# Causal attention in groups of four: values one run of turns later, half moves by GpSimd copies, the scaling multiplication one event earlier

## The chip, the cores and the metric

One Trainium2 chip, one core. The metric is the device time of one execution in microseconds (us); lower is better. Times before come from three timed runs, and one further execution was profiled.

## The reference

One layer of a decoder: half a SwiGLU feed-forward step, a mixing step of three branches, half a second feed-forward step. There are 1024 positions of width 1024, all in float32. The change lies in branch B, causal attention with 8 heads, 96 query and key dimensions and 64 value dimensions:

```python
def one_block(args):
    i, qi = args
    s = jnp.einsum('bqhd,bkhd->bhqk', qi, k).astype(jnp.float32) * scale
    qpos = i * Q_BLOCK + jnp.arange(Q_BLOCK)
    mask = kpos[None, :] <= qpos[:, None]
    s = jnp.where(mask[None, None], s, NEG)
    p = jax.nn.softmax(s, axis=-1)
    return jnp.einsum('bhqk,bkhd->bqhd', p.astype(v.dtype), v)
```

## The kernel before

Float32 products are made of split numbers: a matrix is cut into a high part (`hi`, an ACT copy with rounding) and a low part (`lo`, the rest, a subtraction on DVE or POOL); `split` on L139 and L142 does both.

The attention works head by head on blocks of 128 positions. Query blocks are taken in two groups of four: group 0 is blocks 0 to 3 and group 1 is blocks 4 to 7. The steps are:

- R, one step of `prepare`: four transposes of queries or keys on PE (L450) into a PSUM bank, evicted by ACT (L150) and DVE (L151). Four such steps serve a head. For each pair of heads two 768 KB tiles, `ak` and `aq`, are loaded (L972).
- S or N, `scores` of one query block: PE writes the products into a tile `mm` (two of these exist, L158 to L160), DVE adds the mask and finds the extreme (L998), and ACT takes the exponential with its sum (L1001) into `pr`.
- T, `turn` of one key block: up to four transposes of `pr` (L1011) into one PSUM `bank` (there are four, which R and the value sums use too), evicted by `split` into `whi` (ACT) and `wlo` (DVE). For the last key block of a group POOL clears a corner (L1016).
- V, `value` of one key block: two matmuls (L1027, with `whi` and with `wlo`) that add to one bank over the whole group. The weights hold the values' high and low halves side by side, so the upper and the lower 64 rows of the sum must be added.
- `close`, after the last value of a group: ACT copies the sum to a tile `t` (L1043), the half that sits in the wrong rows is moved (L1044), and POOL adds the other half (L1045) into `ysum`, which gathers two heads. For an odd head DVE takes the reciprocals of the softmax sums (L1048). They go to DRAM as 4 KB (L1063, `invd`) and come back spread over 64 rows each (L1065, two loads to a tile `t`). A function put into the list `late` multiplies `ysum` by them on POOL (L1068) and splits the result: `x<-ysum` on ACT (L139) and POOL (L142). `late` counts events, that is, closes of a group.

A "cycle" of a head is written out by hand in `cycle(h)`; in it group 1 of the head before (TB, VB) and group 0 of this head (TA, VA) are interleaved with scores. Only PE follows the written order exactly. For the other engines and the DMA queue on SP, a scheduler fixes an order when the program is built; each engine then runs its own list in order and waits on semaphores.

## Time and profile before

| | |
|---|---|
| three timed runs | 2209.91, 2211.65 (median), 2212.57 us |
| profiled execution | 2212.67 us, span in the trace 2210.9 us |
| TensorE busy | 2175.1 us (98%), mean granted clock 0.994 |
| attention cycles | about 1251 to 1446 us of the span |

The span is cut off from the time by 1.77 us around it. In the trace each row has a start, a duration, an engine, a line and, in brackets, how long the engine had been idle before it and what ended that. PE's busy time runs to the modelled end of each matmul, so some waiting hides in it.

### The profile page before, as it was taken

To read this page: it belongs to the slowest core of one execution; us is meant where nothing else is said; L and a number is where in the kernel's file an instruction comes from. 1 tells how busy PE (TensorE), PEld (TensorE's weight loads), DVE (VectorE), ACT (ScalarE), POOL (GpSimd) and SP (SyncE) were. 2 spreads that over 40 slices of the span, in tenths; PEclk is the share of its full clock that TensorE was granted. 3 is DMA by queue.
4 is the path that set the end of the run, shared out by engine and by line. 5 is a ranking of instruction groups with operands and counts; after the bars stand their busy time and mean duration, and the time that the engine had idled before them with its cause. 6 is when DMAs were issued, how large, how long until landed. Compare 5 with 4: busy or idle time off the path is not lost.

```text
span 2210.9 us, 27223 instructions
## 1 busy us (share of the span) xinstructions
PE 2175.1 (98%) x9984; PEld 1798.6 (81%) x9984; DVE 1557.5 (70%) x2350; ACT 907.5 (41%) x1485; POOL 272.6 (12%) x244
## 2 busy tenths in 40 slices
PE   9999999999999999999999988899999999999999
PEld 6888888888888888888888766778888888888887
DVE  7976666589898666665976566585886666657884
ACT  6433333343455344433555366543442222224332
POOL 0011111100000000000313322240011121210000
PEclk9999999999999999999999999899999999999999
DMA  4265555684443445532786712175033333338543
GB/s 144 93 225 175 185 172 186 224 309 147 143 148 138 146 172 183 196 132 72 271 318 229 261 49 51 39 279 197 29 114 101 100 115 100 115 107 299 175 129 105
DMA packets 140870, 352.25 MB, mean 159 GB/s; under 512 B 22208, under 2 KB 30528, under 8 KB 140736
## 3 DMA queue, kind: packets, MB, share of 16 engines
q1 hardware_dynamic: 140592, 350.51, 46.5%
q8 instruction: 78, 1.28, 0.2%
q14 instruction: 56, 0.46, 0.1%
q10 hardware_dynamic: 144, 0.00, 0.0%
HBM read 235.62 MB, written 113.01 MB: 158 GB/s over the span
## 4 chain that ended last, share of the span: by engine, by line
PE 92%; DVE 3%; DMA 2%; ACT 1%; issue 1%; POOL 1%; SPq 0%; POOLq 0%; ACTq 0%; DVEq 0%
PE one L158 15%; PE one L159 15%; PE one L160 15%; PE bank L158 13%; PE bank L159 13%; PE bank L160 13%; PE bank L1027 2%; PE mm L158 1%; PE mm L159 1%; PE mm L160 1%; PE bank L1011 1%; DMA ysum<-t 1%; DVE wlo L142 1%; PE one L1982 1%; PE bank L1982 0%
## 5 line engine op out<-in xcount | busy, mean ns | idle before, releaser
L146 ACT CAST whi<-x 128x1024 fp32r<-128x1024 f32 x202 | 192.2, 955 | 405.0 <-DVE x L1452 162.5
L147 DVE TENSOR_TENSOR wlo<-x,whi 128x1024 fp32r<-128x1024 f32 x202 | 236.8, 1173 | 72.1 <-DMA wkv<-wlo 25.1
L1486 DVE TENSOR_TENSOR t<-t,one 128x512 f32<-128x512 f32 x188 | 128.9, 686 | 182.2 <-PE one L160 182.0
L158 PE MATMUL bank<-h,whi 128*128 128x512 f32 x636 | 248.1, 390 | 0.0
L160 PE MATMUL bank<-h,wlo 128*128 128x512 f32 x636 | 247.6, 389 | 0.0
L159 PE MATMUL bank<-h,whi 128*128 128x512 f32 x636 | 247.5, 389 | 0.0
L158 PE MATMUL one<-h,whi 128*128 128x512 f32 x508 | 198.9, 392 | 0.0
L160 PE MATMUL one<-h,wlo 128*128 128x512 f32 x508 | 198.3, 390 | 0.0
L159 PE MATMUL one<-h,whi 128*128 128x512 f32 x508 | 198.1, 390 | 0.0
L158 PE MATMUL one<-w,whi 128*128 128x512 f32 x432 | 168.5, 390 | 0.0
L160 PE MATMUL one<-w,wlo 128*128 128x512 f32 x432 | 168.1, 389 | 0.0
L159 PE MATMUL one<-w,whi 128*128 128x512 f32 x432 | 168.1, 389 | 0.0
L142 DVE TENSOR_TENSOR wlo<-w,whi 128x1024 fp32r<-128x1024 f32 (+2 forms) x112 | 114.4, 1037 | 65.4 <-ACT whi L139 65.1
L139 ACT CAST whi<-w 128x1024 fp32r<-128x1024 f32 (+2 forms) x112 | 98.8, 902 | 150.1 <-PE one L159 63.9
L2082 POOL TENSOR_TENSOR raw<-raw 128x512 f32<-128x512 f32 x38 | 57.0, 1499 | 796.2 <-DVE raw L1923 702.8
L160 PEld LDWEIGHTS bank<-h,wlo 128*128 128x128 f32 x636 | 119.4, 188 | 25.0
L158 PEld LDWEIGHTS bank<-h,whi 128*128 128x128 f32 x636 | 119.4, 188 | 24.6
L159 PEld LDWEIGHTS bank<-h,whi 128*128 128x128 f32 x636 | 119.4, 188 | 24.5
L158 PE MATMUL bank<-whi 128*128 128x512 f32 x352 | 136.9, 389 | 0.0
L159 PE MATMUL bank<-wlo,whi 128*128 128x512 f32 x352 | 136.9, 389 | 0.0
L160 PE MATMUL bank<-whi,wlo 128*128 128x512 f32 x352 | 136.9, 389 | 0.0
L160 PEld LDWEIGHTS one<-h,wlo 128*128 128x128 f32 x508 | 95.6, 188 | 20.0
(409 smaller groups left out, 4885.6 us busy)
## 6 DMA issues: line engine op xcount, KB each, us to landing
x<-in_ffn_w_gu_dram SPq DMA_DIRECT2D x78, 512.0 KB, 5.1
w<-tdt SPq DMA_DIRECT2D x40, 512.0 KB, 4.5
gate<-raw SPq DMA_DIRECT2D x33, 512.0 KB, 3.0
tdb<-raw SPq DMA_DIRECT2D x64, 256.0 KB, 2.3
h<-in_ffn_w_down_dram SPq DMA_DIRECT2D x64, 256.0 KB, 6.0
w<-tdb SPq DMA_DIRECT2D x30, 512.0 KB, 4.6
tdt<-w SPq DMA_DIRECT2D x48, 256.0 KB, 2.6
x<-in_w_gate_dram SPq DMA_DIRECT2D x22, 512.0 KB, 6.9
```

The costliest lines, as they stand in the source:

```text
L139: i = self.nc.scalar.copy(hi, src)
L142: return (eng or self.nc.vector).tensor_tensor(lo, src, hi.bitcast(F32), op=ALU.subtract)
L146: self.nc.scalar.copy(hi, src)
L147: return lambda: self.nc.vector.tensor_tensor(lo, src, hi.bitcast(F32), op=ALU.subtract)
L158: i = mmul(out, s[0], m[0], start=first, stop=False, **kw)
L159: mmul(out, s[0], m[1], start=False, stop=False, **kw)
L160: self.last = mmul(out, s[1], m[0], start=False, stop=last, **kw)
L1011: nc.tensor.transpose(b[:, t * P:(t + 1) * P], st[h, 4 * g + t][:, kk * P:(kk + 1) * P], self.ident)
L1027: nc.tensor.matmul(o[:, at:], w, x, start=kk == k == 0, stop=kk == 4 * g + 3 and k == 1, skip_group_check=True)
L1486: return self.nc.vector.tensor_tensor(out, x, y, op=ALU.add)
L1982: k.last = nc.tensor.matmul(b, w, norm.x(half, c), start=c == 0, stop=c == DT - 1)
L2082: sub = lambda d, x, y: (eng or nc.gpsimd).tensor_tensor(d, x, y, op=ALU.subtract)
```

## The change

Three edits:

- the half move L1044 is a GpSimd (POOL) copy from one half of the partitions to the other, in place of a DMA on SP's queue (14 of them: heads 0 to 6, two groups; head 7 has another path);
- the `late` function is cut in two: the multiplication is put out after two events and the split after three, where both stood at three;
- in `cycle` each run of values stands behind the next run of turns (or scores), not behind its own.

```diff
                     both = self.row()
                     nc.scalar.copy(both, o)
-                    nc.sync.dma_start(ys[rows], both[other])
+                    nc.gpsimd.tensor_copy(ys[rows], both[other])
                     nc.gpsimd.tensor_tensor(ys[rows], ys[rows], both[rows], op=ALU.add)
...
-                    def scale(y=yt[h // 2], cols=slice(g * 4 * P, (g + 1) * 4 * P)):
-                        nc.gpsimd.tensor_tensor(ys, ys, w, op=ALU.mult)
-                        self.split(y[0][:, cols], y[1][:, cols], ys, None if end else nc.gpsimd)
-
-                    late.append((0 if end else 3, scale))
+                    y, cols = yt[h // 2], slice(g * 4 * P, (g + 1) * 4 * P)
+                    late.append((0 if end else 2, lambda: nc.gpsimd.tensor_tensor(ys, ys, w, op=ALU.mult)))
+                    late.append((0 if end else 3, lambda: self.split(
+                        y[0][:, cols], y[1][:, cols], ys, None if end else nc.gpsimd)))
...
-                    *R(2), *TB(0, 1), *S(4), *VB(0, 1), *TB(2, 3, 4), *S(5), *VB(2, 3, 4), *TB(5, 6, 7), *S(6), *VB(5, 6, 7),
-                    *R(1), *TA(0, 1), *S(7), *VA(0, 1), *R(1), *TA(2, 3), *N(0, 1), *VA(2, 3), *N(2, 3)]
+                    *R(2), *TB(0, 1), *S(4), *TB(2, 3, 4), *S(5), *VB(0, 1), *TB(5, 6, 7), *S(6), *VB(2, 3, 4),
+                    *R(1), *TA(0, 1), *S(7), *VB(5, 6, 7), *R(1), *TA(2, 3), *N(0, 1), *VA(0, 1), *N(2, 3), *VA(2, 3)]
```

On PE, at the end of the first cycle: the rows with `h_10301` to `h_10304` are the values of key blocks 0 to 3, those with `mm` are scores of the next head (N).

```order
 L159 MATMUL mm<-h_10527,h_10524 128x256
 L160 MATMUL mm<-h_10526,h_10525 128x256
-L1027 MATMUL bank<-whi,h_10303 128x256
-L1027 MATMUL bank<-wlo,h_10303 128x256
-L1027 MATMUL bank<-whi,h_10304 128x256
-L1027 MATMUL bank<-wlo,h_10304 128x256
+L1027 MATMUL bank<-whi,h_10301 128x512
+L1027 MATMUL bank<-wlo,h_10301 128x512
+L1027 MATMUL bank<-whi,h_10302 128x384
+L1027 MATMUL bank<-wlo,h_10302 128x384
 L158 MATMUL mm<-h_10526,h_10524 128x384
 L159 MATMUL mm<-h_10527,h_10524 128x384
```

The values of blocks 0 and 1 take the place that blocks 2 and 3 had, and those now follow after two more scores.

On ACT, at the start of the cycle of head 2 (the first with a `x<-ysum`), before:

```order
L150 ACTIVATE h_10908<-bank,g_ev_k 96x512
L1001 ACTIVATE pr_10903,a_rs<-pr_10903,a_mx 128x512
L139 CAST whi<-bank 128x512
L150 ACTIVATE h_10906<-bank,a_gq 96x512
L139 CAST whi<-bank 128x512
L139 CAST x_10364<-ysum 128x512
L139 CAST whi<-bank 128x512 x3
L1001 ACTIVATE pr_10948,a_rs<-pr_10948,a_mx 128x640
```

and now:

```order
L150 ACTIVATE h_10908<-bank,g_ev_k 96x512
L139 CAST whi<-bank 128x512 x2
L150 ACTIVATE h_10906<-bank,a_gq 96x512
L139 CAST whi<-bank 128x512 x3
L139 CAST x_10364<-ysum 128x512
L1001 ACTIVATE pr_10948,a_rs<-pr_10948,a_mx 128x640
```

The cast `x<-ysum` moves from behind the second eviction of a turn to behind the fifth.

On SP's queue, the transfers of heads 0 to 3 before:

```order
L1044 DMA ysum<-t 64x512
L1063 DMA invd<-a_inv 128x8x1
L1044 DMA ysum<-t 64x512
L1063 DMA invd<-a_inv 128x8x1
L1065 DMA t<-invd 64x512 x2
L1044 DMA ysum<-t 64x512
L1065 DMA t<-invd 64x512
L1044 DMA ysum<-t 64x512
L1065 DMA t<-invd 64x512
L972 DMA ak<-kd 128x1536
L972 DMA aq<-qd 128x1536
```

and now:

```order
L1063 DMA invd<-a_inv 128x8x1 x2
L1065 DMA t<-invd 64x512 x2
L972 DMA ak<-kd 128x1536
L1065 DMA t<-invd 64x512 x2
L972 DMA aq<-qd 128x1536
```

The moves of halves are gone from the queue; both stores of reciprocals still stand ahead of the first group's loads, and the second group's loads now stand between `ak` and `aq`.

## The prediction

> **What bounds the kernel now.** I read the page first, then the attention by cycles of a head, then its waits, then single rows.

> ```profile
> PE 2175.1 (98%) x9984; PEld 1798.6 (81%) x9984; DVE 1557.5 (70%) x2350; ACT 907.5 (41%) x1485; POOL 272.6 (12%) x244
> ```

> TensorE (PE) is the bound of the whole, but the change touches only the attention. Cut there at the copies L1043 that close group 0 of heads 0 to 6 (columns: length, then busy us of PE, PEld, DVE, ACT, POOL, then the granted clock):

> ```profile
> core 0: us, PE busy (x) PEld busy (x) DVE busy (x) ACT busy (x) POOL busy (x), PEclk, DMA share, GB/s
> 1269.10:1291.20 22.10, 19.59 (x117) 15.68 (x116) 14.84 (x35) 14.63 (x35) 3.19 (x6) 1.00 0.17 32
> 1291.20:1318.00 26.80, 19.92 (x111) 15.93 (x110) 14.72 (x32) 15.72 (x38) 8.26 (x10) 0.94 0.26 78
> 1318.00:1340.00 22.00, 19.03 (x114) 15.17 (x113) 14.80 (x34) 14.75 (x35) 3.18 (x6) 1.00 0.14 21
> 1340.00:1363.80 23.80, 20.00 (x117) 15.79 (x116) 14.62 (x33) 15.66 (x37) 8.28 (x10) 1.00 0.31 93
> 1363.80:1386.40 22.60, 19.77 (x111) 15.86 (x110) 14.70 (x34) 14.78 (x36) 3.19 (x6) 0.92 0.12 20
> 1386.40:1413.30 26.90, 22.25 (x113) 17.93 (x112) 14.68 (x32) 15.91 (x37) 8.30 (x10) 0.85 0.10 26
> 1413.30:1433.50 20.20, 18.80 (x92) 15.38 (x92) 11.67 (x26) 11.54 (x26) 4.72 (x10) 0.84 0.20 65
> ```

> I call these cycles 1 to 7. Cycles 2, 4 and 6 are longer: in them the sums of a finished pair of heads are scaled and split. No engine is full, so the cycles are set by waits:

> ```profile
> POOL ysum L1045 <- DMA ysum<-t: 85.1, 9, 13.7
> PEld bank L1027 <- DVE wlo L142: 36.5, 60, 1.6
> PE bank L1027 <- DVE wlo L142: 19.1, 29, 1.3
> ACT x L139 <- POOL ysum L1068: 15.9, 6, 5.9
> PE bank L1027 <- ACT whi L139: 8.2, 13, 3.2
> ```

> PE waits at the values alone, 19.1 + 8.2 = 27.3 us, for the split of the turns just before them. What PE's work would take without waits comes from starts of rows in cycle 3:

> ```profile
> 1319.02 0.60 PE L450 MATMUL bank<-ident,ak 128*96 128x128 f32 x4
> 1319.45 0.60 PE L450 MATMUL bank<-ident,aq 128*96 128x128 f32 x4
> 1323.95 1.47 PE L1011 MATMUL bank<-ident,pr 128*128 128x128 f32 x12
> 1325.18 0.48 PE L158 MATMUL mm<-h,h 96*128 96x512 f32 x1
> 1325.73 0.40 PE L160 MATMUL mm<-h,h 96*128 96x512 f32 x1
> 1325.96 0.28 PE L158 MATMUL mm<-h,h 96*128 96x256 f32 x1
> ```

> Four transposes of R take 0.43 us, a transpose of a turn 1.23 / 12 = 0.10 us, a pass of 512 columns 0.23 us. A cycle has 16 transposes of R, 36 of turns, 14,592 columns of scores in three passes and 9,728 of values: 1.7 + 3.7 + (24,320 / 512) x 0.23 = 16.3 us; with 0.3 us for short passes 16.6 us. Cycle 3 thus holds 22.0 - 16.6 = 5.4 us of waiting.

> The three long cycles have a stall of their own. In cycle 2:

> ```profile
> 1287.56 0.37 SPq L1063 DMA_DIRECT2D invd<-a_inv  x1
> 1288.03 1.18 SPq L1065 DMA_DIRECT2D t<-invd  x2
> 1291.79 0.48 SPq L1044 DMA_DIRECT2D ysum<-t  x1
> 1298.54 1.26 POOL L1045 TENSOR_TENSOR ysum<-ysum,t 64x512 f32<-64x512 f32 x1 [11.97 <-DMA ysum<-t]
> 1299.88 1.26 POOL L1068 TENSOR_TENSOR ysum<-ysum,t 128x512 f32<-128x512 f32 x1
> 1301.18 0.62 ACT L139 CAST x<-ysum 128x512 fp32r<-128x512 f32 x1 [5.91 <-POOL ysum L1068]
> 1302.33 0.49 PE L1027 MATMUL bank<-whi,h 128*128 128x512 f32 x1 [3.23 <-ACT whi L139]
> ```

> ACT stood 5.91 us at `x<-ysum`, and PE 3.23 us for want of the eviction behind it. The views of the transfers around those issues (last column: us to landing) tell what was late:

> ```profile
> invd<-a_inv SPq DMA_DIRECT2D x1, 4.0 KB, 9.7
> t<-invd SPq DMA_DIRECT2D x2, 128.0 KB, 9.7
> ysum<-t SPq DMA_DIRECT2D x1, 128.0 KB, 6.6
> ysum<-t SPq DMA_DIRECT2D x1, 128.0 KB, 2.2
> DMA to landing us min/median/max: 8.2/9.0/10.5
> ```

> The last line is that of all six stores of reciprocals. The store issued at 1287.56 lands at 1297.3, the loads behind it by 1298.3, and the half move, which elsewhere takes 2.2 us, at 1298.4. So two things arrived together: the moved half, which the change takes off the queue, and the reciprocals, which it doesn't.

> **The change part by part.** *The half moves.* Out: 14 issues on SP; in: 14 copies on POOL. No row shows a POOL copy that crosses partitions. The nearest are

> ```profile
> L471 POOL COPY k<-h 128x512 f32<-128x512 f32 x4 | 2.9, 734 | 0.0
> L1045 POOL TENSOR_TENSOR ysum<-ysum,t 64x512 f32<-64x512 f32 x14 | 17.8, 1272 | 125.4 <-DMA ysum<-t 85.1 <-ACT whi L139 18.9 <-DMA t<-invd 11.8
> L1043 ACT COPY t<-bank 128x512 f32<-128x512 f32 x14 | 8.2, 583 | 7.2 <-PE bank L1027 7.2
> ```

> so 0.73 us (a copy of as many columns) to 1.27 us (two inputs); I take 0.73, since it too reads one input. Of POOL's 22 to 27 us a cycle at most 8.3 are busy, and nobody waits for the copy except the add and the multiplication. Queued behind it on POOL are the corner clears, which the value of the last block needs; that value now runs later. Cost nothing, up to some 5 us a copy, while the reciprocals are as late as above. The 85.1 us that POOL waited are no gain, as POOL is no bound.

> *The chain of reciprocals.* In long cycles the sum is now closed (copy 0.58 + 0.73 + 1.27) about 3 us into the cycle. The multiplication then waits for loads that stand on SP, as before, behind the store of the second group, and that store waits for the exponential of the last score. Before: store at 1287.56, loads landed at 1298.3, L1045 and L1068, cast at 1301.18, 13.6 us after the store. Now only L1068 follows the loads: cast 12.3 us after the store. ACT reaches the cast three evictions later, that is about 6 us into a cycle instead of 3 to 4; the cast can go at about 10 to 11, since the reciprocals are taken late in the shorter cycle. So ACT still stands about 4 us, but the five turns behind which the values wait are evicted, and PE loses some 2.7 us of a cycle instead of all that the stall holds back.

> *The values one step later.* What PE waits for moves from its own split to the banks: R twice, then turns 0 and 1 fill the four banks, and turns 2 to 4 need them evicted. Per step the rows give

> ```profile
> L142 DVE TENSOR_TENSOR wlo<-bank,whi 128x512 fp32r<-128x512 f32 x48 | 31.5, 685 | 13.1 <-ACT whi L139 12.2 <-issue 0.8
> L139 ACT CAST whi<-bank 128x512 fp32r<-128x512 f32 x48 | 26.2, 582 | 10.9 <-PE bank L1011 10.9
> ```

> and I walked one short cycle by hand in the new orders of PE, ACT and DVE with the durations of such groups. PE then waits about 1.3 us for banks at turns 2 to 4, 0.7 at turns 6 and 7, 0.5 at the last R and turn 3, and 0.6 at scores 1 to 3 of the next head, for `mm` tiles: 16.6 + 3.1 = 19.7 us. The walk leaves out hand-overs between engines; I add 0.5 us a cycle for them below. A long cycle comes to 19.7 + 2.7 = 22.4.

> *The sum*, against the profiled 2212.67 us: cycles 1, 3, 5: 22.1 + 22.0 + 22.6 - 3 x 19.7 = 7.6. Cycles 2, 4, 6: 26.8 + 23.8 + 26.9 - 3 x 22.4 = 10.3. Cycle 7 has neither R nor the next head's scores; there I take 2. The first scores and the last group: 0.5 each. Together 20.9; less 8 x 0.5 for hand-overs, 16.9. The stage behind has PE busy all through, so the shift passes on unchanged. 2212.67 - 16.9 = 2195.8. The median of the timed runs is 1.0 us lower, so 2195; its own range is 2189 to 2202. *The clock* is in this only where stalled cycles end:

> ```profile
> 1412.25 0.58 PE L1027 MATMUL bank<-wlo,h 128*128 128x256 f32 x1 [0.88 <-DVE wlo L142]
> 1414.00:1418.00 4.00, 4.00 (x15) 3.41 (x15) 2.16 (x6) 2.27 (x6) 1.56 (x3) 0.50 0.15 33
> ```

> Over cycles 2 to 7, (1 - clock) x length is 26.8 x 0.06 + 22.6 x 0.08 + 26.9 x 0.15 + 20.2 x 0.16 = 10.7 us. The row shows the clock at half with PE busy throughout, after idle spells no longer than 0.88 us just before. If PE runs denser the clock may hold, and some of the 10.7 comes back.

> [...]

> **The rivals.**

> *The clock comes back.* Some 8 of the 10.7 us are added to the 16.9, of which two or three are counted already in the long cycles: about 23 to 28, so 2186. For it: PE would be 84% dense instead of 75%. Against: the long cycles keep a stall.

> *The long cycles stay as long.* If the reciprocals land still later (store at the end of a cycle, 10.5 us, then the loads), ACT stands 6 us at the cast and the 10.3 falls to about 3: gain 9.6, so 2202. For it: the six stores' 8.2 to 10.5 us are untouched.

> *The banks take it all.* PE waits at the turns for exactly the evictions for which it waited at the values; all of the 27.3 us could reappear at L1011. No change, 2212, if turns 2 to 4 wait through to the second R step.

> *Slower: banks.* The sum's bank is taken after turn 4 and held to the next run, so that turns 5 to 7 have three banks for the evictions of 2 to 4. If turns 2 to 4 wait 1.9 us longer than in the walk and turns 5 to 7 1.5 us, 8 x 3.4 = 27 us eat the 16.9 and leave +10 us, 2222. It decides from 2.1 us a cycle. Against: DVE evicts the banks in the order in which the turns ask for them, and is busy only 15 of 22 us.

> **How the numbers follow.** Chances: my forecast 0.42, the clock 0.16, long cycles as long 0.18, banks take all 0.12, slower 0.12. Within 0.2% (4.4 us, about what a measurement of this kernel can tell from no change) is the fourth: faster 0.76, same 0.12, slower 0.12. The range goes from 2184 (the clock in full) to 2212 (banks take all) and leaves out the slower case and little below.

> **What would show it.** In the trace after: L1044 on POOL, near 0.73 us; cycles of 20 us (odd) and 22 to 23 us (even), PE near 84% of them; the waits of L1027 for `wlo` a few us instead of 19.1, and waits of L1011 for DVE in their place, near 2 us a cycle; `x<-ysum` on ACT still waiting 3 to 5 us in cycles 2, 4 and 6. Waits at L1011 above 4 us a cycle, a copy of over 5 us, or a wait of ACT above 8 us would make the prediction wrong.

## The result, and the profile after

The changed kernel takes 2181.70 us (median of four runs, 2179.47 to 2182.66) against 2212.11 us (2209.91 to 2213.99) for the kernel before on the same chip: a ratio of 0.9861, with a 95% interval of 0.9844 to 0.9879. The forecast was 2195 with a range of 2184 to 2212: the sign was right, but the time lies below the range, with a gain of 30.4 us where the sum had 16.9. The profiled execution took 2181.63 us (span 2179.9).

First the cycles of the changed kernel, cut at the same copies L1043; the last row is the end with the last group (columns as before: length, busy us of PE, PEld, DVE, ACT, POOL, then the granted clock):

```profile
1268.10:1286.20 18.10, 18.00 (x115) 15.24 (x114) 14.32 (x35) 14.98 (x35) 4.49 (x8) 1.00 0.05 0
1286.20:1308.90 22.70, 19.69 (x114) 16.54 (x113) 14.09 (x33) 15.21 (x35) 8.19 (x11) 0.92 0.30 94
1308.90:1327.30 18.40, 18.02 (x114) 15.20 (x113) 14.39 (x35) 15.30 (x35) 5.71 (x9) 1.00 0.05 2
1327.30:1348.00 20.70, 18.78 (x115) 15.27 (x114) 14.11 (x33) 15.46 (x36) 8.18 (x11) 1.00 0.35 103
1348.00:1366.40 18.40, 18.02 (x115) 15.21 (x113) 14.39 (x35) 15.32 (x36) 5.71 (x9) 1.00 0.05 1
1366.40:1389.60 23.20, 19.67 (x114) 16.35 (x112) 14.11 (x33) 15.19 (x36) 8.17 (x11) 0.93 0.19 69
1389.60:1403.90 14.30, 13.79 (x87) 11.72 (x86) 10.19 (x24) 11.47 (x26) 5.03 (x10) 1.00 0.00 1
1403.90:1413.70 9.80, 7.71 (x48) 6.01 (x47) 8.62 (x17) 8.24 (x17) 3.55 (x6) 1.00 0.16 48
```

Cycles 1, 3 and 5 fell from 22.0 to 22.6 us to 18.1 to 18.4, cycles 2, 4 and 6 from 23.8 to 26.9 to 20.7 to 23.2, cycle 7 from 20.2 to 14.3. DVE and ACT do about as much as before; what went is waiting. One part of cycle 7 is no gain: the copy that ends a cycle now stands behind the scores of query blocks 2 and 3 of the next head (the last `N(2, 3)` in the diff), where it stood ahead of them. For cycles 1 to 6 this changes nothing, as each gives one such pair away and takes one in. But cycle 7, which has no next head, has lost a pair without taking one: 2,688 columns of passes, some 1.2 us at 0.23 us for 512 columns. The stretch ahead of cycle 1 has taken that work in. The waits of the changed kernel that answer to those shown of before (sum, times, longest):

```profile
PE bank L1027 <- DVE wlo L142: 0.8, 1, 0.8
PE bank L1027 <- ACT whi L139: 1.1, 1, 1.1
PEld bank L1011 <- DVE wlo L142: 5.3, 21, 0.5
ACT whi L139 <- PE bank L1011: 1.2, 2, 0.8
PE bank L450 <- DVE wlo L142: 7.5, 3, 3.4
POOL ysum L1068 <- DMA t<-invd: 18.4, 3, 7.1
ACT x L139 <- POOL ysum L1068: 15.5, 4, 5.8
```

The 27.3 us that PE waited at the values are 1.9 now. They did not come back at the banks: L1011 waits 5.3 us for DVE's split in all. ACT used to wait for PE's turns as well, and that went with it; this is the row of the kernel before that answers to the fourth one above:

```profile
ACT whi L139 <- PE bank L1011: 24.3, 16, 2.3
```

Before, PE stood until DVE had split a turn, and then ACT stood until PE had made the next. With the values one run later both work at once. The run with the new order of values alone, below, shows the same 0.8 and 1.1 us at L1027, so this is the work of that edit. What is left is the stall at `x<-ysum`, 5.22, 3.44 and 5.75 us in cycles 2, 4 and 6, and PE's wait behind it, now at the third step R. In the changed kernel's trace:

```profile
1269.66 15.49 SPq L1063 DMA_DIRECT2D invd<-a_inv  x2
1285.21 1.22 SPq L1065 DMA_DIRECT2D t<-invd  x2
1295.34 1.28 POOL L1068 TENSOR_TENSOR ysum<-ysum,t 128x512 f32<-128x512 f32 x1 [6.55 <-DMA t<-invd]
1296.65 0.62 ACT L139 CAST x<-ysum 128x512 fp32r<-128x512 f32 x1 [5.22 <-POOL ysum L1068]
1299.11 1.09 PE L450 MATMUL bank<-ident,ak 128*96 128x128 f32 x4 [2.90 <-DVE wlo L142]
1379.81 0.64 PE L450 MATMUL bank<-ident,ak 128*96 128x128 f32 x4 [3.42 <-DVE wlo L142]
```

The first row groups both stores of reciprocals: one at 1269.66, the other ends at 1285.15, and the loads of the first group stand behind both.

### The profile page after: what moved, and what is told of

Same layout as the page of the kernel before. It is cut to its first block, busy times and chain, and to the rows that moved or that the text cites. A ratio compares the mean times of both kernels' runs of the same rounds, so it can differ in the third digit from the quotient of the medians.

```text
span 2179.9 us, 27187 instructions
## 1 busy us (share of the span) xinstructions
PE 2160.1 (99%) x9984; PEld 1792.7 (82%) x9984; DVE 1554.0 (71%) x2350; ACT 907.9 (42%) x1485; POOL 281.5 (13%) x258
## 5 line engine op out<-in xcount | busy, mean ns | idle before, releaser
L147 DVE TENSOR_TENSOR wlo<-x,whi 128x1024 fp32r<-128x1024 f32 x202 | 237.0, 1174 | 72.2 <-DMA wkv<-wlo 24.9
L158 PE MATMUL bank<-h,whi 128*128 128x512 f32 x636 | 248.1, 390 | 0.0
L160 PE MATMUL bank<-h,wlo 128*128 128x512 f32 x636 | 247.6, 389 | 0.0
L158 PE MATMUL one<-h,whi 128*128 128x512 f32 x508 | 198.9, 392 | 0.0
L160 PE MATMUL one<-h,wlo 128*128 128x512 f32 x508 | 198.4, 391 | 0.0
L158 PE MATMUL one<-w,whi 128*128 128x512 f32 x432 | 168.6, 390 | 0.2 <-DVE t L1485 0.2
L160 PE MATMUL one<-w,wlo 128*128 128x512 f32 x432 | 168.1, 389 | 0.0
L142 DVE TENSOR_TENSOR wlo<-w,whi 128x1024 fp32r<-128x1024 f32 (+2 forms) x112 | 114.4, 1037 | 66.2 <-ACT whi L139 66.0
L139 ACT CAST whi<-w 128x1024 fp32r<-128x1024 f32 (+2 forms) x112 | 98.8, 901 | 149.7 <-PE one L159 63.1
L160 PEld LDWEIGHTS bank<-h,wlo 128*128 128x128 f32 x636 | 119.4, 188 | 24.9
L158 PEld LDWEIGHTS bank<-h,whi 128*128 128x128 f32 x636 | 119.4, 188 | 24.5
L158 PE MATMUL bank<-whi 128*128 128x512 f32 x352 | 136.9, 389 | 0.0
L160 PE MATMUL bank<-whi,wlo 128*128 128x512 f32 x352 | 136.9, 389 | 0.0
L160 PEld LDWEIGHTS one<-h,wlo 128*128 128x128 f32 x508 | 95.7, 188 | 20.0
```

Source lines behind the costliest of these rows:

```text
L139: i = self.nc.scalar.copy(hi, src)
L142: return (eng or self.nc.vector).tensor_tensor(lo, src, hi.bitcast(F32), op=ALU.subtract)
L147: return lambda: self.nc.vector.tensor_tensor(lo, src, hi.bitcast(F32), op=ALU.subtract)
L158: i = mmul(out, s[0], m[0], start=first, stop=False, **kw)
L160: self.last = mmul(out, s[1], m[0], start=False, stop=last, **kw)
```

## The experiments

Each run was compared with the kernel before on the chip that it ran on, where that took 2214.8 to 2216.9 us (median), so ratios are compared between runs and not times.

**The three edits apart.** First the new order of values alone:

```diff
-                    *R(2), *TB(0, 1), *S(4), *VB(0, 1), *TB(2, 3, 4), *S(5), *VB(2, 3, 4), ...
+                    *R(2), *TB(0, 1), *S(4), *TB(2, 3, 4), *S(5), *VB(0, 1), *TB(5, 6, 7), ...
```

> The kernel before with only the new order of values in the cycle; half moves stay DMAs, multiplication and split stay at three events. Theory A (the gain of 30 us is the values: PE no longer waits at L1027, and the clock holds): 2181 to 2188, PE waits at L1027 under 5 us, short cycles near 18.4 us. Theory B (the half moves as DMAs hold up the long cycles, the queue matters as much as the order): about 2195, short cycles 18.4 us but long cycles at 24 to 27 us as before.

Then the copies alone:

```diff
-                    nc.sync.dma_start(ys[rows], both[other])
+                    nc.gpsimd.tensor_copy(ys[rows], both[other])
```

> The kernel before with only the half moves as POOL copies. Theory A: the reciprocals land at the same moment as the moved half did, so only the add of 1.3 us leaves the chain in three long cycles: 2206 to 2210, short cycles 22 us as before. Theory B: 2198 to 2203, long cycles shorter by 3 us or more.

Copies and the earlier multiplication, values in the old order:

```diff
+                    late.append((0 if end else 2, lambda: nc.gpsimd.tensor_tensor(ys, ys, w, op=ALU.mult)))
```

> The kernel before with POOL copies and the multiplication one event sooner, values in the old order. Theory A: like the copies alone, 2206 to 2210, as the multiplication waits for the reciprocals whichever event puts it out. Rival: the multiplication put out sooner frees the cast on ACT, 2198 to 2204, waits of ACT for L1068 falling from 15.9 to under 8 us.

And values and copies, with the multiplication back at three events:

```diff
-                    late.append((0 if end else 2, lambda: nc.gpsimd.tensor_tensor(ys, ys, w, op=ALU.mult)))
+                    late.append((0 if end else 3, lambda: nc.gpsimd.tensor_tensor(ys, ys, w, op=ALU.mult)))
```

> The changed kernel with multiplication and split both at three events again. Theory A: the same time as the changed kernel within 2 us, 2180 to 2184, since ACT and SP have the same lists in the long cycles. Rival (the sooner multiplication carries part of the gain): 2185 to 2190.

Measured, with the kernel before at 2215.38 us: values alone 2196.08 us, ratio 0.9918 (0.9898 to 0.9938); copies alone 2205.24, 0.9960 (0.9948 to 0.9972); copies and multiplication 2206.16, 0.9961 (0.9942 to 0.9979); values and copies 2184.03, 0.9862 (0.9846 to 0.9879). So the earlier multiplication is worth nothing, in either order of values. The values bring 19.3 us and the copies 10.1 alone and 12.0 on top of the values. For the values theory B came out in the main: their short cycles take 18.0 to 19.9 us, but their long ones 25.8, 22.5 and 24.9. The copies alone came out just below the 2206 to 2210 of theory A, and the chain did what that theory says: ACT's wait at `x<-ysum` fell from 15.9 to 12.0 us, three times the add of 1.3. On top of the values the copies take more out: there PE waits 14.0 us for DVE's split at L450 without them and 7.5 with them.

The copies alone leave short cycles without a slow stretch as they were (22.1 and 22.0 us). Most of their gain lies where the kernel before ran at a lower clock. These are cycles 6 and 7 with the copies alone, which stand against 26.9 us at 0.85 and 20.2 us at 0.84 before:

```profile
1385.30:1408.60 23.30, 19.34 (x114) 15.21 (x113) 14.52 (x32) 15.75 (x37) 9.58 (x12) 1.00 0.17 58
1408.60:1426.50 17.90, 16.28 (x92) 12.72 (x91) 11.67 (x26) 11.43 (x26) 5.90 (x12) 1.00 0.00 0
```

**What the stall is made of.** The store of the second group's reciprocals goes to ACT's queue, in the changed kernel:

```diff
-                        nc.sync.dma_start(dst.rearrange("o (t p) -> p o t", p=P), rs)
+                        (nc.scalar if g else nc.sync).dma_start(dst.rearrange("o (t p) -> p o t", p=P), rs)
```

> The changed kernel, in which the store of the second group's reciprocals is issued from ACT's queue instead of SP's; nothing else differs. In the changed kernel the loads for the first group are issued 0.4 us behind that store and the multiplication sees them 10 us later, though their own store was issued 15 us before. Theory 'queue': the loads stand behind the other store on SP's queue. Then they land within 3 us of their issue, x<-ysum on ACT no longer stands 5.2, 3.4 and 5.8 us in cycles 2, 4 and 6, each of these cycles falls from 22.7, 20.6 and 23.2 to near 19, and the kernel takes 2171 to 2175. Rival 'engines': the 1024 small packets of the store occupy the DMA engines whichever queue they came from; the loads land as late as now and the time stays within 2 us of 2182. Rival 'issue': ACT pays for the issue in front of the exponentials of the next head, 0.4 us three times: 2183.

2169.28 us, ratio 0.9792 (0.9776 to 0.9807): faster than both kernels, and somewhat below the 2171 to 2175 of theory 'queue'. The chip's time before was 2216.87 us. In the timeline of this run the loads are issued ahead of the second store, and ACT's cast does not wait:

```profile
1281.79 1.09 SPq L1065 DMA_DIRECT2D t<-invd  x2
1285.34 0.37 ACTq L1063 DMA_DIRECT2D invd<-a_inv  x1
1291.88 0.62 ACT L139 CAST x<-ysum 128x512 fp32r<-128x512 f32 x1
```

Its view of transfers gives those loads 2.8 us to landing. And in the windows a long cycle takes what a short one does, at full clock:

```profile
1286.70:1304.80 18.10, 18.00 (x114) 15.22 (x113) 14.09 (x33) 15.46 (x36) 8.20 (x11) 1.00 0.33 102
```

As the loads now go ahead of the store, this run alone doesn't tell the theories 'queue' and 'engines' apart. (Cycles 3 and 5 take 18.4 and 18.8 us here: in them PE waits up to 1.0 us for the load of `aq`.)

The reciprocals kept on the chip, for all heads as for the last one, with no store and no load:

```diff
-                    if end:
+                    if True:
                         b = self.bank()
...
-                    else:
-                        dst = sums[h // 2, g]
-                        nc.sync.dma_start(dst.rearrange("o (t p) -> p o t", p=P), rs)
```

> The changed kernel, in which the reciprocals of all heads go the way of the last head: spread by two GpSimd copies, turned by four transposes on PE into a bank, copied out by ACT; no store and no loads. Theory 'reciprocals': what cycles 2, 4 and 6 are longer than 1, 3 and 5 is the wait for the reciprocals' transfers; they fall to near 19 each, PE has no gap over 1.3 us, no spell at half clock is left in the attention, and the time is 2170 to 2175. Rival 'work': the long cycles are long by the work of scaling (three more instructions on ACT and POOL each), and the added 8 transposes, 4 copies and 2 evictions a pair make it 2182 to 2185.

2176.17 us, ratio 0.9824 (0.9809 to 0.9839): better than the change, and just outside both expectations. The stall is gone, but each long cycle pays for the turn of the reciprocals with 8 transposes and 2 evictions:

```profile
1284.60:1305.30 20.70, 19.12 (x123) 16.17 (x122) 14.12 (x33) 16.69 (x39) 9.43 (x14) 1.00 0.22 77
```

The copy made dearer, each one done four times:

```diff
+                    for _ in range(4):
-                    nc.gpsimd.tensor_copy(ys[rows], both[other])
+                        nc.gpsimd.tensor_copy(ys[rows], both[other])
```

> The changed kernel with each half move copied four times over, so 2.4 us on POOL instead of 0.61, 1.8 us more at each of 14 places. The prediction held that a copy of up to 5 us costs nothing, since the multiplication waits for the reciprocals. Theory 'free': 2182 within 2 us. Rival 'in the chain': the 1.8 us show where POOL is waited for, in cycles 2, 4 and 6: 2184 to 2188. Rival 'everywhere': the corner clears behind the copies hold turns in all cycles up: over 2190.

2176.15 us, ratio 0.9825 (0.9808 to 0.9843), so faster than with one copy, which no theory held. POOL did the added work (56 copies of 621 ns). But the scheduler had put the cast at another place of ACT's list: at the end of the cycle, two rows ahead of the closing copy at 1302.72, instead of behind the fifth eviction. There its row shows no wait:

```profile
1301.60 0.60 ACT L139 CAST x<-ysum 128x512 fp32r<-128x512 f32 x1
```

And the window of that cycle, a long one:

```profile
1284.60:1302.70 18.10, 17.98 (x115) 15.26 (x113) 14.12 (x33) 15.18 (x35) 9.17 (x15) 1.00 0.36 117
```

So it doesn't test the price of a copy by itself. It speaks for another thing: that the long cycles are long because evictions queue on ACT behind a cast whose input is late, and not because the scaled sum is needed sooner.

**Is it the queue, or what lies behind it?** The store on ACT's queue again, with the half moves left as transfers on SP: with the new order of values, and in the kernel before with nothing else changed. The diff is that of the store above.

> The kernel before with the new order of turns and values and with the second group's reciprocal store on ACT's queue; the half moves stay transfers on SP. It asks what the copies are worth once nothing slow stands ahead of the transfers. Theory 'queue': the half moves were dear only because they landed behind that store (6.6 us instead of 2.2); then x<-ysum waits under 1 us in all cycles, all cycles take 18 to 18.6, and the ratio to the kernel before is 0.979 to 0.982, that of the changed kernel with the same store. Rival 'hop': a transfer of 2.2 us against a copy of 0.61 keeps the sum and so the cast late by itself: 1.5 us in each long cycle and half a us in the others, ratio 0.983 to 0.987.

> The kernel before with nothing changed but the second group's reciprocal store, on ACT's queue. Theory 'stall and values add up': the stall of 5.9, 3.3 and 4.2 us at x<-ysum goes, cycles 2, 4 and 6 fall to 22 to 22.5, the waits at the values stay (19 + 8 us in all), and with a spell or two less at half clock the kernel is 8 to 14 us faster (ratio 0.994 to 0.9965). Rival 'values hide it': without the stall PE waits at the values for the splits behind the cast instead, and less than 4 us comes out (ratio over 0.998).

Ratios 0.9896 (0.9879 to 0.9912; 2191.15 against 2215.04 us) and 0.9997 (0.9986 to 1.0008; 2213.51 us). The first lies outside both of its expectations, because the half move was held up there as well: it is issued 2.0 us behind the store on ACT's queue (1283.85), and POOL, which waits for it, can add only 8.6 us later. From that run's timeline:

```profile
1285.84 0.48 SPq L1044 DMA_DIRECT2D ysum<-t  x1
1294.43 1.28 POOL L1045 TENSOR_TENSOR ysum<-ysum,t 64x512 f32<-64x512 f32 x1 [9.53 <-DMA ysum<-t]
```

The second ratio lies where its rival put it, but not for the rival's reason: the stall had not gone. In this second kernel's timeline the half move of the second group is issued on SP 4.2 us behind the store on ACT's queue, and the sum and the cast wait as long as ever:

```profile
1285.37 0.37 ACTq L1063 DMA_DIRECT2D invd<-a_inv  x1
1289.58 0.48 SPq L1044 DMA_DIRECT2D ysum<-t  x1
1297.00 1.26 POOL L1045 TENSOR_TENSOR ysum<-ysum,t 64x512 f32<-64x512 f32 x1 [12.66 <-DMA ysum<-t]
1299.64 0.62 ACT L139 CAST x<-ysum 128x512 fp32r<-128x512 f32 x1 [6.58 <-POOL ysum L1068]
```

Its view of transfers gives that half move 7.3 us to landing, where 2.2 are usual. So here the half move is counted as landed 0.4 us after the store (issued at 1285.37, 11.1 us to landing), though it stands on the other queue. The changed kernel with the store on ACT's queue is fast because the loads are issued 3.6 us ahead of the store (1281.79 against 1285.34) and land in 2.8 us, and because the half move, a copy of 0.61 us on POOL, is no transfer. The last combination, copies and that store in the old order (again both edits shown above):

> The kernel before with the copies and with the second group's reciprocal store on ACT's queue; turns and values in the old order. The store alone brought nothing, and the half move issued 4 us behind it still took 7.3 us though it was on another queue: so what follows the store on any queue is held up. Theory 'held transfers': with copies no transfer is left behind the store but the next heads' loads, x<-ysum does not stand at all, the long cycles fall to the 22 us of the short ones, and the ratio is 0.989 to 0.992. Rival 'old order': without the new order PE waits for the splits behind the cast anyway and the ratio stays that of the copies alone, 0.995 to 0.997.

0.9938 (0.9922 to 0.9955; 2201.54 against 2214.84 us), between the two expectations. No cast waits, and the long cycles are as long as the short ones (22.5 and 21.6 us). The third column from the end shows that the clock was not full in the first of them. The short cycles 3 and 5 take 24.1 and 23.0 us here, at clocks of 0.88 and 0.93, so slow stretches hide part of the gain:

```profile
1289.30:1311.80 22.50, 19.64 (x110) 15.91 (x109) 14.36 (x32) 15.91 (x38) 9.57 (x12) 0.90 0.24 83
1335.80:1357.40 21.60, 19.12 (x114) 15.26 (x114) 14.43 (x32) 15.14 (x34) 9.59 (x12) 1.00 0.24 70
```

All ratios to the kernel before, by where the second store is issued:

| | store on SP | store on ACT |
|---|---|---|
| old order, transfers | 1 | 0.9997 |
| old order, copies | 0.9960 | 0.9938 |
| new order, transfers | 0.9918 | 0.9896 |
| new order, copies | 0.9861 | 0.9792 |

The store's place is worth nothing that these runs can tell to the kernel before and 0.7%, 15 us, to the changed one. (The ratios' intervals reach some 0.0011 to 0.002 to each side.)

**The clock.** Idle work on PE in the kernel before, ahead of the values at which it waits:

```diff
+                if kk == 0:
+                    for _ in range(5):
+                        nc.tensor.transpose(o[:, :P], self.ident, self.ident)
+                if kk in (2, 5):
+                    at, w, x = again
+                    for _ in range(2):
+                        nc.tensor.matmul(o[:, at:], w, x, start=False, stop=False, skip_group_check=True)
```

> The kernel before, with idle work put on PE just ahead of the places where it waits: five transposes of the identity into the sum's bank ahead of the first value of a group, and two repeats of a product of the last turn ahead of values 2 and 5 (these add to the sum, so the output is another). About 0.5 us of PE work at each place, none of it needed. Theory 'density': the spells at half clock follow a stretch of 3.4 us in which PE was busy less than about 2 us; with 0.4 us more in each such stretch the spells near 1381, 1398, 1408 and 1432 go, only the one behind the long stall of cycle 2 stays, and the kernel is 3 to 9 us faster although it does more. Rival 'waits only': the clock falls by something else and the gain of the change is all from waits; then the spells stay, and the added work makes it 0 to 15 us slower.

2216.34 us, ratio 1.0006 (0.9996 to 1.0017). Half of each expectation came true. The slow stretches went as the density theory says: of those near 1303, 1381, 1398, 1408 to 1419 and 1432 us two are left, one behind each of two long stalls, and (1 - clock) x length summed over the attention falls from 11.9 to 3.4 us. This is no chance of one execution: the mean clock is 0.996 to 0.998 in all ten runs, against 0.991 to 0.995 in the 13 of the kernel before on that chip. But the work that brought this costs as much: clean short cycles take 22.8 us instead of 22.0 to 22.1. Cycle 7 takes 19.0 us at full clock, where it took 20.2. Cycle 3 of this run:

```profile
1320.40:1343.20 22.80, 20.09 (x130) 17.31 (x129) 14.70 (x34) 14.75 (x35) 3.18 (x6) 1.00 0.13 24
```

**What sets the 18 us.** The fastest version with five idle transposes ahead of each group's first value:

```diff
+                if kk == 0:
+                    for _ in range(5):
+                        nc.tensor.transpose(o[:, :P], self.ident, self.ident)
```

> The changed kernel with the second group's store on ACT's queue (as in store_act, which took 2169.28 with every cycle at 18 us and PE busy in 17.9 of them), and with five transposes of the identity into the sum's bank ahead of the first value of each group: 16 x about 0.5 us of PE work that nothing needs. It asks what sets the 18 us now. Theory 'PE': PE has no wait left, so the 0.5 us come through in full, each cycle is 1.0 us longer and the kernel 7 to 9 us slower than store_act (ratio to before 0.982 to 0.984). Rival 'banks and splits': if PE still waits inside the cycle for banks, as the prediction walked it (3.1 us a cycle), the added work sits in those waits and 0 to 3 us come out (ratio 0.979 to 0.981).

2170.99 us, ratio 0.9799 (0.9784 to 0.9813), 0.9792 without. About 1.0 us of work a cycle makes a cycle some 0.55 us longer (18.05 to 18.60); the ratios differ by 0.0007, some 1.6 us, where six such cycles alone would give 3.3; the intervals allow both. Neither theory holds whole: at these two places PE has about 0.45 us of slack in a cycle of which the profile calls 18.0 busy:

```profile
1285.10:1303.70 18.60, 18.58 (x125) 16.41 (x123) 14.15 (x33) 15.23 (x37) 8.22 (x11) 1.00 0.30 98
```

## Why the prediction was right in sign and wrong in size

By its own terms, from the starts of L1043 and L1039 in the two profiles:

| term | forecast | measured |
|---|---|---|
| cycles 1, 3, 5 | 7.6 | 11.8 |
| cycles 2, 4, 6 | 10.3 | 10.9 |
| cycle 7 | 2 | 5.9 |
| first scores | 0.5 | 1.0 |
| last group | 0.5 | 2.6 |
| hand-overs | -4.0 | 0 |
| behind the attention | 0 | -1.2 |
| sum | 16.9 | 31.0 |

The scores that left cycle 7 shift some 1.2 us between two measured rows: for equal work cycle 7 gained about 4.7 and the first scores about 2.2. The -1.2 behind the attention says that the shift did not pass on whole; no run takes that up.

**The walked short cycle was the step that failed.** It had 16.6 us of dense work, 3.1 us of waits and 0.5 for hand-overs: 20.2. Measured are 18.1 to 18.4, in cycles 1 and 3 without a slow stretch before or after. The term that was too large is the 3.1 us of waits. The walk had PE wait 1.3 us at turns 2 to 4 and 0.7 at turns 6 and 7; in cycle 1 of the changed kernel the starts are

```profile
1270.81 1.85 PE L1011 MATMUL bank<-ident,pr 128*128 128x128 f32 x12
1272.41 0.48 PE L158 MATMUL mm<-h,h 96*128 96x512 f32 x1
1274.46 1.06 PE L1011 MATMUL bank<-ident,pr 128*128 128x128 f32 x6
1275.28 0.48 PE L158 MATMUL mm<-h,h 96*128 96x512 f32 x1
```

The twelve transposes of turns 2 to 4 take 1272.41 - 1270.81 = 1.60 us, 0.4 more than the 1.23 without waits, and the six of turns 5 to 7 take 0.82 where 0.6 would do, 0.2 more. Read in the same way turn 3 is 0.2 late instead of 0.5, and the scores of the next head 0.2 instead of 0.6. That is 1.0 us in place of 3.1. (In cycle 3 turns 2 to 4 lose 0.7 us, which makes 1.3.) The rest of the 18.1 us, 17.1, is the dense work, a little more than the 16.6 of the prediction: a first pass behind transposes takes 0.32 us (to its next start, 1272.73) instead of 0.23.

Why the walk waited too long is in part an argument, as the prediction doesn't write out its single steps. It chained full durations on ACT and DVE. The changed kernel's cycle 3 shows that the next instruction starts before the row of the last one ends:

```profile
1311.21 1.07 ACT L139 CAST whi<-bank 128x512 fp32r<-128x512 f32 x2
1312.17 0.70 ACT L150 ACTIVATE h<-bank,a_gq 96x512 fp32r<-96x512 f32 x1
1315.03 1.28 DVE L142 TENSOR_TENSOR wlo<-bank,whi 128x512 fp32r<-128x512 f32 x2
1316.23 0.94 DVE L998 CUSTOM_DVE_ANT_0 pr<-mm,mask 128x768 f32<-128x768 f32 x1
```

Two casts that the walk counted as 2 x 0.582 = 1.16 us leave ACT free after 1312.17 - 1311.21 = 0.96. Two subtractions counted as 2 x 0.685 = 1.37 leave DVE free after 1316.23 - 1315.03 = 1.20. Each step was thus counted 0.1 us or so too long, and an estimated ten of them in a row would make up 1 of the 2 us; the rest stays open. The hand-over allowance, an estimate that no row shows, added 0.5 a cycle in the same wrong direction. The waits predicted for L1011, near 2 us a cycle, are 5.3 us in all.

**The long cycles' term came out right by luck, through two errors.** The stall on ACT was forecast at about 4 us and is 5.22, 3.44 and 5.75. The reason given, loads behind the second store, holds too. But what a stall takes from PE was set at 2.7 us on top of a cycle that was 1.4 too long. Measured, the three cycles exceed a short one by 3.9 us on average, 22.2 less 18.3.

**Cycle 7 and the last group were guessed, and the clock was in them.** Cycle 7 ran at 0.84 before and at 1.00 after. With the copies alone it takes 17.9 us at full clock, so by that run 2.3 of the 5.9 us are the slow stretch and 3.6 the values, of which some 1.2 are the scores that moved out. The last group gives 0.9 of its 2.6 in the same way (11.57 us with the copies alone, 12.44 before). The sum had put the clock at nothing, though the prediction itself had 10.7 us of it in view: that is its second failed term.

**The rivals.** "The clock comes back" was the nearest, at 2186. (1 - clock) x length fell from 11.9 to 3.4 us over the attention. What that is worth can be read from the spread of the kernel before: over 7 to 13 timed runs of it on each of four chips the time rises by 0.52, 0.58, 0.66 and 0.81 us for each us of (1 - clock) x span. The 8.5 us are then 4 to 7 us of time, of the 14 that the sum was short. That is an estimate; the run with idle work on PE, which should have measured it, gave the clock back and took about as much for its own work. "The long cycles stay as long" falls with their 10.9 us. Both rivals of the banks fall with the 5.3 us at L1011.

**The small prices.** A copy took 607 ns where 0.73 us was taken, and cost nothing. That up to some 5 us a copy would be free was not tested, since in the run with four copies ACT's order moved too. The sooner multiplication had no price in the sum, rightly: it is worth nothing (0.9861 with it, 0.9862 without). The copies were costed at no gain beyond the 1.3 us that the add leaves the chain of reciprocals. That much they take off the chain, but they bring 10 to 12 us. Part of it is the held transfer, which a copy is not (in the kernel before a half move took 4.5 to 6.6 us in the long cycles, where it stands behind a store, and 2.2 to 2.4 elsewhere); another part lies in stretches where the clock was lower before and is full with the copies. No run separates the two.

## What to carry to other kernels

Where two engines stop for each other in turn (PE for DVE's split, then ACT for PE's next turn), one more run of work between producer and user can take out the waits of both at once (here 27.3 us at PE's values fell to 1.9, and 24.3 us at ACT to 1.2). A cast, store or load whose input comes late should not stand in a list ahead of work that others wait for: here a later place on ACT (2176.15 us), an earlier issue on SP (2169.28) and a way without transfers (2176.17) each removed the same stall, and the cheapest was to move one store to another queue. When cycles are walked by hand, take steps from start to start of neighbouring rows, not from durations.

## What the runs showed of the hardware

**In these runs a half move issued 4 to 5 us behind a small store landed just after it, on either queue.** The transfers' view of the kernel before with the store on ACT's queue, from 1285 to 1298 us in 40 slices of 0.325 us: the share of the DMA engines that were busy, then the packets of SP's queue (q1) and of ACT's (q10).

```profile
DMA  0000770000000000049400070000000000000003
q1 hardware_dynamic: 98, 0.17, 5.4%
q10 hardware_dynamic: 1040, 0.00, 3.6%
invd<-a_inv ACTq DMA_DIRECT2D x1, 4.0 KB, 11.1
```

The store's 1040 packets pass in the two slices from 1286.3, and the half move's in those from 1290.5 to 1291.5. (The busy slice at 1292.5 is one packet of the instruction queue.) Yet the store counts as landed 11.1 us after its issue, at 1296.5, and the half move at 1296.9: for 5 us no packet of either moves and neither is counted as landed. In the kernel before, with all of them on SP's queue, the half moves issued 4.2, 4.2 and 5.4 us behind the stores of 1287.56, 1336.41 and 1381.60 us landed 1.1, 0.4 and 0.3 us after those. Why a half move lands no sooner than the store, and the store itself only some 10 us after its packets, no run shows.

```profile
1299.36:1302.77 3.41, 0.44 (x1) 0.19 (x1) 0.46 (x1) 1.59 (x4) 2.60 (x3) 1.00 0.02 5
1302.77:1306.18 3.41, 3.18 (x10) 2.53 (x10) 1.80 (x4) 1.30 (x3) 0.81 (x4) 0.50 0.00 0
1394.93:1398.34 3.41, 1.74 (x6) 0.82 (x6) 1.89 (x3) 2.90 (x6) 1.96 (x5) 1.00 0.00 0
1398.34:1401.75 3.41, 3.41 (x12) 2.94 (x12) 2.02 (x5) 1.94 (x5) 0.00 (x0) 0.50 0.00 0
1309.60:1313.01 3.41, 2.11 (x10) 1.20 (x7) 2.51 (x5) 2.60 (x6) 1.27 (x2) 1.00 0.65 153
1313.01:1316.42 3.41, 2.69 (x17) 2.17 (x17) 1.42 (x5) 2.57 (x7) 2.60 (x3) 1.00 0.59 207
```

A window with PE busy 1.74 of 3.41 us was followed by half clock, one with 2.11 was not; between 1.59 and 2.02 us both were seen (1.59 was followed by full clock with the values alone, 2.02 by half clock in the kernel before). The windows at half clock from 1408.58 and 1411.99 have PE busy 2.79 and 3.15 us and were followed by half clock again; that from 1302.77, with 3.18, was followed by full clock. In the changed kernel's trace the two stretches begin at 1299.08 and 1381.00, 24 x 3.41 apart, but 3.69 us from 1302.77, which is no multiple. That the windows lie elsewhere in each execution, so that which of two equal cycles is hit differs from run to run, is an estimate from these two traces. It would explain why the kernel before spreads over 9 us in 11 runs (2210.44 to 2219.39 on one chip); only the profiled runs show where the stretches begin, so it isn't shown. The prediction's gap of 0.88 us ahead of 1414 lies inside the stretch that began at 1408.58; the window ahead of that has PE busy 1.98 us, 58% of it, and no gap above 1.27.
